# Closing norm of a two-layer recurrent decoder step: three sums into one bank and one root, a spread without a diagonal, two scalings moved behind the last sum

## Chip, core and metric

One Trainium2 chip, one of its cores. The metric is the device time of one execution in microseconds. Engines are named as in the profile: PE (TensorE matmul), PEld (its weight load), DVE (VectorE), ACT (ScalarE), POOL (GpSimd), SP (SyncE). ACTq and SPq are the queues of ACT and SP on which DMAs are issued. "L1797" is line 1797 of the kernel.

## The reference, cut to what matters

1024 prompt tokens and 8 x 4 sample tokens go through two layers of width 1024: an RG-LRU block, then an HGRN2 block. Both layers end in an output projection and a residual add, and after the second comes one more RMS norm:

```python
def _rmsnorm(x, gain):
    xf = x.astype(jnp.float32)
    y = xf * lax.rsqrt(jnp.mean(xf * xf, axis=-1, keepdims=True) + EPS)
    return (y * gain.astype(jnp.float32)).astype(x.dtype)
...
    return x + y @ w_out, S_T.astype(x.dtype)
...
    return _rmsnorm(x, final_gain), jnp.stack(hs), jnp.stack(bufs), jnp.stack(Ss)
```

The change touches only this last norm, for the last of the tokens.

## The kernel before, in words

Activations lie transposed: 128 features on the partitions, tokens along the free dimension, 1056 tokens (TOK) in a row. The width of 1024 is eight such tiles, called m (or k) = 0 to 7 below. fp32 products are made of three matmuls with operands split into a high and a low part (`mm3`, L266 to L268).

The second layer, with its output projection and the last norm, is recorded into one planner (`Flow`). Each call of `fl.add`, `act`, `dve`, `pool`, `pe` or `dma` records an operation with an engine, an estimated duration, the keys that it reads and writes and a priority. `Flow.run` then makes a list schedule, improves it by passes from the end and by a random search, and emits the operations in the order it found. Each engine then runs its own instructions strictly in that order, and waits on semaphores for the others. A DMA is issued by SP, or by ACT for odd tiles, and takes its place in that engine's order.

The projection's last three eighths of the inner dimension are done at the very end, span by span. `OUT` has three spans of tokens: 512, 288 and 256. For each span and each m:

- PE makes nine matmuls into one of three PSUM banks (`mm`);
- DVE adds that to the residual in SBUF (L1797);
- ACT squares the new x (L1799);
- the squares are summed over the eight m: for the first two spans on POOL, by adding to an accumulator (L1808). In the last span m = 1, 2 and 3 go that way, and from m = 4 on PE sums directly.

The sum over the 128 partitions is a matmul with the accumulator (or a square) as weights and one column of ones as the moving operand (`norm_sum`, L303). It gives one number for each token, with 128 tokens on the partitions. One such matmul is needed for each 128 tokens of the span, so two for the last span, each into a bank of its own. In the last span there are five rounds of them: the accumulator (m = 0 to 3), then the squares of m = 4, 5, 6 and 7.

`roots` takes a square root for each column (ACT, L1740), a reciprocal for all (DVE, L1743), and multiplies an identity by the result, so that the numbers stand on a diagonal (DVE, L1744, and L1748 for the rest that is no multiple of 128). `spread` multiplies ones by that diagonal on PE (L1754): each partition then holds the factor of every token. `finish` scales the eight tiles of x by the gain and the factor and stores them. DVE does five of them in one instruction each, from the PSUM bank (L1774). For the other three (k = 5, 6, 7) ACT copies the bank to SBUF (L1767), ACT multiplies x by the gain (L1771) and POOL by the copy (L1772). The store of each tile is a DMA (L336): even k on SP, odd k on ACT. The program lets one engine at a time read a bank of PSUM: DVE's first scaling, ACT's copy and DVE's next scaling of a span wait for one another.

The scaling of a span is placed inside the next one: its sums are made when the next span stands at m = 3 (`RM`), its spread and scaling at m = 6 (`SM`). So the 288 span is scaled while the 256 span's last products run. After the last sums two idle matmuls (`spin`, L1812) are recorded, then the roots, spread and scaling of the last span, which have nothing beside them.

In profile names, x of the last stage is `ST` for k = 0, `R` for k = 1, 2, 3, `a` (a_114) for k = 4 and `sg` (sg_147, sg_145, sg_149) for k = 5, 6, 7. The squares go to other parts of tiles `a` (a_115) and `sg` (sg_150), the accumulator is in `R`, the copy of the factors is in `sg` (sg_146), the roots are `nr`.

Of the kernel before, what the change touches and what calls it, by code (L numbers as in the profile page):

```python
# [19 lines left out]
ALU = mybir.AluOpType  # L20
# [214 lines left out]
def tile_trunk(ctx: ExitStack, tc: tile.TileContext, xT, prm, hc, w0, wg, wo0, w1, wo1, s_in,  # L235
# [64 lines left out]
    def norm_sum(sums, acc, n, start, stop):  # L300

        for s, (a, u) in zip(sums, spans(n)):
            T.matmul(s[:u], acc[:, a:a + u], ones[:, :1], start=start, stop=stop)  # L303

# [663 lines left out]
    with ExitStack() as l1:  # L968
# [787 lines left out]

        def summed(acc, ak, n):
# [5 lines left out]
        def finish(a, n, bc, bk):  # L1763
            q = slice(a, a + n)
            own = KD - 3 if a else KD
            if a:
                act(n, lambda: S.copy(sb[0][:, :n], bc), (bk,), (sb[1],), 0)  # L1767
            for k in (*range(own, KD), *range(own)):
                x, xk = x2[k][:, q], ykeys(Y2 + k, a, n)
                if k >= own:  # L1770
                    act(n, lambda x=x, k=k: S.activation(x, x, AF.Copy, scale=pc("gf", k)), xk, xk, 1)  # L1771
                    pool(n, lambda x=x: G.tensor_tensor(x, x, sb[0][:, :n], op=ALU.mult), (sb[1], *xk), xk, 1)  # L1772
                else:
                    dve(n, lambda x=x, k=k: V.scalar_tensor_tensor(x, x, pc("gf", k), bc, op0=ALU.mult, op1=ALU.mult), (bk, *xk), xk, 1)  # L1774
                dma(yT[k][:, q], x, xk, (), 1, n / 2, S if k % 2 else Q)

        for a, n in OUT:
# [4 lines left out]
            for m in range(KD):  # L1782
                if a and m == RM:
                    dg = summed(*prev[:2], prev[3])
                if a and m == SM:
                    finish(*prev[2:], *spread(prev[3], *dg, True))
# [13 lines left out]
                if final and m >= 4:  # L1800
                    if m == 4:
                        sums = [(next(hg)) for _ in spans(n)]
                        sumk = [k for _, k in sums]
                        sums = [s[:, :1] for s, _ in sums]
                        fl.add("PE", 0.3, lambda acc=acc, n=n, sums=sums: norm_sum(sums, acc, n, True, False), (ak,), sumk, 0)
                    fl.add("PE", 0.3, lambda sq=sq, n=n, m=m, sums=sums: norm_sum(sums, sq, n, False, m == KD - 1), (sk, *sumk), sumk, 0)
# [4 lines left out]
        for _ in range(2):  # L1811
            fl.add("PE", 0.45, lambda: T.matmul(spin[:, :128], ones, ones, start=True, stop=True), sumk, (wk,), 0)  # L1812
        finish(a, n, *spread(n, *roots(n, sums, sumk), False))
# [73 lines left out]
```

## Time and profile before

| what | value |
|---|---|
| median of 3 runs | 1031.88 us (1031.04 to 1032.02) |
| profiled execution, its own time | 1033.11 us |
| its span, first to last instruction | 1031.3 us |
| busy share of the span: PE, DVE, ACT, POOL | 99%, 78%, 56%, 48% |
| mean granted clock of TensorE | 0.996 |

The span leaves out what lies ahead of the first and behind the last instruction, 1.81 us in this execution. Its time is 1.23 us above the median of the runs without a profile. Busy times of PE are modelled, so 99% says that PE is seldom without a matmul, not that it is at its peak. In the rows of a timeline the columns are start, duration, engine, line, operation, what it writes and reads, its shape, and in brackets how long the engine was idle before it and what ended that. "x2" is two merged instructions; an fp32 matmul appears as two matmuls.

### The profile page before, as it was taken

How to read it: one execution, taken by the hardware profiler on the slowest of the kernel's cores; microseconds unless marked ns; L12 is line 12 of the kernel's file. 1: busy time of each engine (PE TensorE's matmuls, PEld its weight loads, DVE VectorE, ACT ScalarE, POOL GpSimd, SP SyncE). 2: the span in 40 equal slices, each digit the busy share in tenths (PEclk: the TensorE clock that was granted, in tenths of full speed). 3: DMA queues.
4: the chain of work that ended last, by engine and by line, in shares of the span. 5: the costliest groups of instructions: out<-in, count | busy, mean ns of one | idle time of the engine just before them, and what ended most of it. 6: DMA issues, size and time to landing. Idle time of an engine off the chain costs nothing.

```text
span 1031.3 us, 26510 instructions
## 1 busy us (share of the span) xinstructions
PE 1019.6 (99%) x10134; PEld 998.2 (97%) x10134; DVE 804.9 (78%) x1641; ACT 579.8 (56%) x1326; POOL 496.4 (48%) x573
## 2 busy tenths in 40 slices
PE   9999999999999999999999999999999999999997
PEld 9999999999999999999999999999999999999986
DVE  7998785779798779335598999787989798986436
ACT  8787645876765776335354373626263636552333
POOL 0216353544435255635525555555565557633544
PEclk9999999999999999999999999999999999999998
DMA  8211112223661477526564244443635353686204
GB/s 295 83 29 56 59 50 73 62 62 104 211 211 59 138 253 252 158 92 210 166 189 134 69 154 131 130 142 111 167 111 168 104 162 119 206 243 208 88 1 168
DMA packets 109582, 139.95 MB, mean 136 GB/s; under 512 B 24208, under 2 KB 86800, under 8 KB 109456
## 3 DMA queue, kind: packets, MB, share of 16 engines
q1 hardware_dynamic: 107152, 135.50, 42.8%
q10 hardware_dynamic: 2304, 2.77, 0.8%
q8 instruction: 79, 1.29, 0.5%
q14 instruction: 47, 0.39, 0.1%
HBM read 90.02 MB, written 41.61 MB: 128 GB/s over the span
## 4 chain that ended last, share of the span: by engine, by line
PE 84%; DVE 5%; ACT 4%; DMA 3%; issue 2%; SPq 1%; POOL 0%; ACTq 0%; POOLq 0%; DVEq 0%
PE mm L266 24%; PE mm L267 24%; PE mm L268 24%; PE hg L1101 2%; PE hg L266 1%; PE hg L268 1%; PE hg L267 1%; SPq L336 1%; PE hg L1248 1%; PE hg L1303 1%; DMA R<-td 1%; DMA k<-yd 1%; PE hg L1305 1%; DVE R L628 1%; DMA wraw<-in_w_dram 1%
## 5 line engine op out<-in xcount | busy, mean ns | idle before, releaser
L266 PE MATMUL mm<-xh,whi 128*128 128x352 f32 (+1 forms) x1127 | 350.2, 311 | 0.3 <-DVE k L1561 0.2
L268 PE MATMUL mm<-xh,wlo 128*128 128x352 f32 (+1 forms) x1127 | 347.5, 308 | 0.0
L267 PE MATMUL mm<-xl,whi 128*128 128x352 f32 (+1 forms) x1127 | 347.4, 308 | 0.0
L350 POOL TENSOR_TENSOR wlo<-wraw,whi 128x256 fp32r<-128x256 f32 (+3 forms) x188 | 201.7, 1090 | 210.2 <-ACT whi L409 99.9
L266 PEld LDWEIGHTS mm<-xh,whi 128*128 128x128 f32 x1127 | 212.0, 188 | 1.7 <-issue 0.4
L267 PEld LDWEIGHTS mm<-xl,whi 128*128 128x128 f32 x1127 | 212.6, 189 | 0.7 <-DVE xl L350 0.3
L268 PEld LDWEIGHTS mm<-xh,wlo 128*128 128x128 f32 x1127 | 211.8, 188 | 0.0
L266 PE MATMUL mm<-t,whi 128*128 128x264 f32 (+1 forms) x330 | 96.6, 293 | 0.0
L268 PE MATMUL mm<-t,wlo 128*128 128x264 f32 (+1 forms) x330 | 94.5, 286 | 0.0
L267 PE MATMUL mm<-t,whi 128*128 128x264 f32 (+1 forms) x330 | 94.3, 286 | 0.0
L530 DVE SCALAR_TENSOR_TENSOR k<-xb,prm_sb,k 128x352 f32<-128x352 f32 (+2 forms) x144 | 83.1, 613 | 11.5 <-ACT k L527 10.2
L1561 DVE TENSOR_TENSOR k<-mm,k 128x264 f32<-128x264 f32 x154 | 64.1, 424 | 11.7 <-PE mm L268 10.5
L350 POOL TENSOR_TENSOR wlo<-R,whi 128x256 fp32r<-128x256 f32 x70 | 57.5, 841 | 28.4 <-ACT whi L1485 25.2
L1485 ACT CAST whi<-wraw 128x512 fp32r<-128x512 f32 x56 | 34.6, 618 | 57.9 <-DVE wraw L1495 31.2
L266 PEld LDWEIGHTS mm<-t,whi 128*128 128x128 f32 x330 | 62.0, 188 | 1.3
L409 ACT CAST whi<-wraw 128x512 fp32r<-128x512 f32 (+2 forms) x79 | 43.9, 571 | 33.0 <-PE mm L267 18.0
L267 PEld LDWEIGHTS mm<-t,whi 128*128 128x128 f32 x330 | 62.2, 188 | 0.0
L268 PEld LDWEIGHTS mm<-t,wlo 128*128 128x128 f32 x330 | 62.1, 188 | 0.0
L623 POOL TENSOR_TENSOR k<-X 128x352 f32<-128x352 f32 x36 | 42.5, 1188 | 37.4 <-DVE R L624 26.9
L266 PE MATMUL mm<-yh,whi 128*128 128x352 f32 x153 | 50.0, 327 | 1.5 <-DVE k L675 0.7
L268 PE MATMUL mm<-yh,wlo 128*128 128x352 f32 x153 | 49.4, 323 | 0.0
L267 PE MATMUL mm<-yl,whi 128*128 128x352 f32 x153 | 49.4, 323 | 0.0
(465 smaller groups left out, 2513.6 us busy)
## 6 DMA issues: line engine op xcount, KB each, us to landing
wraw<-in_w_dram SPq DMA_DIRECT2D x88, 256.0 KB, 3.1
wraw<-in_wo_dram SPq DMA_DIRECT2D x34, 192.0 KB, 2.6
R<-in_w_dram SPq DMA_DIRECT2D x17, 256.0 KB, 3.3
si<-in_s_in_dram SPq DMA_DIRECT2D x8, 512.0 KB, 4.7
vt<-sg SPq DMA_DIRECT2D x8, 512.0 KB, 4.4
kt<-kt SPq DMA_DIRECT2D x8, 512.0 KB, 3.8
sg<-vt SPq DMA_DIRECT2D x32, 128.0 KB, 3.1
kt<-kt SPq DMA_DIRECT2D x32, 128.0 KB, 4.8
```

What stands on the lines that cost most here:

```text
L266: T.matmul(out, wh, xh, start=first, stop=False)
L267: T.matmul(out, wh, xl, start=False, stop=False)
L268: T.matmul(out, wl, xh, start=False, stop=last)
L336: fl.add("SP" if q is Q else "ACT", us, lambda: q.dma_start(dst, src), r, w, prio, kb * (1.0 if r else 0.75))
L350: emit = lambda: e.tensor_tensor(b, x, a.bitcast(F32), op=ALU.subtract)
L409: act(m, lambda hi=hi, raw=raw, m=m: S.copy(hi[:, :m], raw[:, :m]), rk, (hk,), prio)
L530: dve(u, lambda src=src, dst=dst, sh=sh, k=k: V.scalar_tensor_tensor(dst, sh(src, k), pc("cw", 12 * k + m), dst, op0=ALU.mult, op1=ALU.add ...
L623: pool(CH, lambda x=x, a=a, b=b: G.tensor_tensor(x, a.bitcast(F32), b.bitcast(F32), op=ALU.add), (ak, bk), (xk,), 3)
L628: dve(3 * CH, lambda ta=ta, ab=ab: V.scalar_tensor_tensor(ta, ab, 1.0, ta, op0=ALU.add, op1=ALU.mult), (*tak, *(("a", s, j) for j in range ...
L1101: T.matmul(ps[32 * j:32 * j + 32, n * w:n * w + w], B[:, o:o + 32], q(slice(o, o + 32)), start=True, stop=True, tile_position=(0, 32 * j))
L1485: act(512, lambda: S.copy(hi, raw), (rk,), (hk,), 2)
L1561: dve(QT, lambda: V.tensor_tensor(o[0], z[0], u[0], op=ALU.add), (z[1], u[1]), (o[1],), 0)
```

## The change

For the 256 span, `last_sum` replaces the five rounds of `norm_sum` by three: the accumulator now takes m = 0 to 5, so POOL adds the squares of m = 4 and 5 as well, and PE sums only the accumulator, m = 6 and m = 7. Both halves of the span go to two columns of one bank. So one square root of 128 x 2 replaces two of 128 x 1. The diagonal falls away: `spread_last` takes the column of roots itself, repeated 128 times, as weights and the identity as the moving operand, in two matmuls of 128 tokens.

In the 288 span, DVE's scalings of k = 3 and 4 are held until x of m = 7 of the 256 span has been added. For the last span POOL's three tiles are now k = 2, 3, 4 instead of 5, 6, 7. The spread's bank of the 288 span changes too, since fewer banks are taken for sums.

```diff
--- before.py
+++ after.py
@@ -302,6 +302,11 @@
         for s, (a, u) in zip(sums, spans(n)):
             T.matmul(s[:u], acc[:, a:a + u], ones[:, :1], start=start, stop=stop)
 
+    def last_sum(s, acc, n, first, last):
+
+        for i, (a, u) in enumerate(spans(n)):
+            T.matmul(s[:u, i:i + 1], acc[:, a:a + u], ones[:, :1], start=first and not i, stop=last, skip_group_check=True)
+
     def new_acts():
         hs, ls = [], []
         for k in range(KD):
@@ -1754,25 +1759,42 @@
             fl.add("PE", 0.002 * n, lambda: T.matmul(bc[:, :n], ones, dg, start=True, stop=True), (dk,), (bk,), 0, main=main)
             return bc[:, :n], bk
 
+        def spread_last(n, r, rk):
+
+            bc, bk = next(hg)
+
+            def emit():
+                for i, (a, u) in enumerate(spans(n)):
+                    T.matmul(bc[:, a:a + u], r[:, i:i + 1].to_broadcast([128, 128]), ident, start=True, stop=True)
+
+            fl.add("PE", 0.0035 * n, emit, (rk,), (bk,), 0)
+            return bc[:, :n], bk
+
         def summed(acc, ak, n):
             s, sk = next(hg)
             sums = [s[:, i:i + 1] for i in range(4)]
             fl.add("PE", 0.7, lambda: norm_sum(sums, acc, n, True, True), (ak,), (sk,), 0, main=True)
             return roots(n, sums, (sk,))
 
-        def finish(a, n, bc, bk):
+        def scaled(k, q, a, n, bc, bk, after=()):
+
+            x, xk = x2[k][:, q], ykeys(Y2 + k, a, n)
+            dve(n, lambda: V.scalar_tensor_tensor(x, x, pc("gf", k), bc, op0=ALU.mult, op1=ALU.mult), (bk, *xk, *after), xk, 1)
+            dma(yT[k][:, q], x, xk, (), 1, n / 2, S if k % 2 else Q)
+
+        def finish(a, n, bc, bk, others, now):
             q = slice(a, a + n)
-            own = KD - 3 if a else KD
-            if a:
+            own = [k for k in range(KD) if k not in others]
+            if others:
                 act(n, lambda: S.copy(sb[0][:, :n], bc), (bk,), (sb[1],), 0)
-            for k in (*range(own, KD), *range(own)):
+            for k in others:
                 x, xk = x2[k][:, q], ykeys(Y2 + k, a, n)
-                if k >= own:
-                    act(n, lambda x=x, k=k: S.activation(x, x, AF.Copy, scale=pc("gf", k)), xk, xk, 1)
-                    pool(n, lambda x=x: G.tensor_tensor(x, x, sb[0][:, :n], op=ALU.mult), (sb[1], *xk), xk, 1)
-                else:
-                    dve(n, lambda x=x, k=k: V.scalar_tensor_tensor(x, x, pc("gf", k), bc, op0=ALU.mult, op1=ALU.mult), (bk, *xk), xk, 1)
+                act(n, lambda x=x, k=k: S.activation(x, x, AF.Copy, scale=pc("gf", k)), xk, xk, 1)
+                pool(n, lambda x=x: G.tensor_tensor(x, x, sb[0][:, :n], op=ALU.mult), (sb[1], *xk), xk, 1)
                 dma(yT[k][:, q], x, xk, (), 1, n / 2, S if k % 2 else Q)
+            for k in own[:now]:
+                scaled(k, q, a, n, bc, bk)
+            return lambda after: [scaled(k, q, a, n, bc, bk, after) for k in own[now:]]
 
         for a, n in OUT:
             q = slice(a, a + n)
@@ -1783,7 +1805,7 @@
                 if a and m == RM:
                     dg = summed(*prev[:2], prev[3])
                 if a and m == SM:
-                    finish(*prev[2:], *spread(prev[3], *dg, True))
+                    rest = finish(*prev[2:], *spread(prev[3], *dg, True), (5, 6, 7) if prev[2] else (), 3 if final else KD)
                 ps, pk = next(mm)
                 hi, lo, wk = late[m]
 
@@ -1797,20 +1819,23 @@
                 dve(n, lambda x=x, ps=ps, n=n: V.tensor_tensor(x, ps[:, :n], x, op=ALU.add), (pk, *xk), xk, 0)
                 sq, sk = next(sqs) if m else (acc, ak)
                 act(n, lambda sq=sq, x=x, n=n: S.activation(sq[:, :n], x, AF.Square), xk, (sk,), 1)
-                if final and m >= 4:
-                    if m == 4:
-                        sums = [(next(hg)) for _ in spans(n)]
-                        sumk = [k for _, k in sums]
-                        sums = [s[:, :1] for s, _ in sums]
-                        fl.add("PE", 0.3, lambda acc=acc, n=n, sums=sums: norm_sum(sums, acc, n, True, False), (ak,), sumk, 0)
-                    fl.add("PE", 0.3, lambda sq=sq, n=n, m=m, sums=sums: norm_sum(sums, sq, n, False, m == KD - 1), (sk, *sumk), sumk, 0)
+                if final and m >= 6:
+                    if m == 6:
+                        sums, sumk = next(hg)
+                        fl.add("PE", 0.45, lambda acc=acc, n=n, sums=sums: last_sum(sums, acc, n, True, False), (ak,), (sumk,), 0)
+                    fl.add("PE", 0.45, lambda sq=sq, n=n, m=m, sums=sums: last_sum(sums, sq, n, False, m == KD - 1), (sk, sumk), (sumk,), 0)
                 elif m:
                     pool(n, lambda acc=acc, sq=sq, n=n: G.tensor_tensor(acc[:, :n], acc[:, :n], sq[:, :n], op=ALU.add), (sk, ak), (ak,), 1)
             prev = acc, ak, a, n
         spin, wk = next(mm)
         for _ in range(2):
-            fl.add("PE", 0.45, lambda: T.matmul(spin[:, :128], ones, ones, start=True, stop=True), sumk, (wk,), 0)
-        finish(a, n, *spread(n, *roots(n, sums, sumk), False))
+            fl.add("PE", 0.45, lambda: T.matmul(spin[:, :128], ones, ones, start=True, stop=True), (sumk,), (wk,), 0)
+        rest(ykeys(Y2 + KD - 1, a, n))
+        w = n // 128
+        r, rk = next(nr2)
+        act(4, lambda: S.activation(r[:, :w], sums[:, :w], AF.Sqrt, bias=epsc, scale=1.0 / D), (sumk,), (rk,), 0)
+        dve(16, lambda: V.reciprocal(r[:, :w], r[:, :w]), (rk,), (rk,), 0)
+        finish(a, n, *spread_last(n, r, rk), (2, 3, 4), KD)
         with tc.manual_schedule(engines={E.PE, E.DVE, E.Activation, E.Pool, E.SP}):
             fl.run(SEARCH, 60.0)
 
```

Everything ahead of the 288 span's scaling stands in the same order as before on all engines, apart from one memset of four columns that falls away on DVE and the order of two DMA issues and an ACT scaling. The order at the end does change, in three places.

On ACT, from the last span's square of m = 5 to the root, before. L1799 are the squares (of sg_147, sg_145, sg_149: m = 5, 6, 7), L1771 the gain on POOL's tiles, L336 the stores of the 288 span (R_73: k = 1 and 3, sg: k = 5 and 7), L1740 the roots:

```order
L1799 ACTIVATE a_115<-sg_147 128x256
L1767 COPY sg_146<-mm_158 128x288
L1771 ACTIVATE sg_147<-sg_147,prm_sb_74 128x256
L336 DMA out_yT_dram<-R_73 128x288
L336 DMA out_yT_dram<-sg_147 128x288
L1799 ACTIVATE a_115<-sg_145 128x256
L1771 ACTIVATE sg_145<-sg_145,prm_sb_74 128x256
L336 DMA out_yT_dram<-R_73 128x288
L1799 ACTIVATE sg_150<-sg_149 128x256
L1771 ACTIVATE sg_149<-sg_149,prm_sb_74 128x256
L336 DMA out_yT_dram<-sg_149 128x288
L1740 ACTIVATE nr20_5315<-hg_164,eps_85 128x1
```

The same stretch of ACT now, where L1821 are the squares, L1789 the copy, L341 the stores and L1836 the root:

```order
L1821 ACTIVATE a_115<-sg_147 128x256
L1789 COPY sg_146<-hg_164 128x288
L341 DMA out_yT_dram<-R_73 128x288
L1821 ACTIVATE a_115<-sg_145 128x256
L341 DMA out_yT_dram<-sg_147 128x288
L1821 ACTIVATE sg_150<-sg_149 128x256
L341 DMA out_yT_dram<-R_73 128x288
L341 DMA out_yT_dram<-sg_149 128x288
L1836 ACTIVATE nr20_5315<-hg_161,eps_85 128x2
```

The three gain scalings have left this stretch (they stand earlier, for k = 2, 3, 4), and one store fewer stands ahead of the square of m = 6. The stores of k = 3 and k = 7 still stand between the last square and the root.

On DVE, from the add of m = 6 (sg_145) to the first scaling of the last span, before. L1797 are the adds, L1774 the scalings:

```order
L1797 TENSOR_TENSOR sg_145<-mm_160,sg_145 128x256
L1774 SCALAR_TENSOR_TENSOR R_73<-R_73,prm_sb_74,mm_158 128x288
L1774 SCALAR_TENSOR_TENSOR a_114<-a_114,prm_sb_74,mm_158 128x288
L1797 TENSOR_TENSOR sg_149<-mm_157,sg_149 128x256
L1743 RECIPROCAL nr20_5315<-nr20_5315 128x2
L1744 TENSOR_TENSOR sg_150<-ident_75,nr20_5315 128x256
L1774 SCALAR_TENSOR_TENSOR ST_143<-ST_143,prm_sb_74,hg_162 128x256
```

And DVE now, with L1819 for the adds and L1782 for the scalings:

```order
L1819 TENSOR_TENSOR sg_145<-mm_160,sg_145 128x256
L1819 TENSOR_TENSOR sg_149<-mm_157,sg_149 128x256
L1782 SCALAR_TENSOR_TENSOR R_73<-R_73,prm_sb_74,hg_164 128x288
L1782 SCALAR_TENSOR_TENSOR a_114<-a_114,prm_sb_74,hg_164 128x288
L1837 RECIPROCAL nr20_5315<-nr20_5315 128x2
L1782 SCALAR_TENSOR_TENSOR ST_143<-ST_143,prm_sb_74,mm_158 128x256
```

The add of m = 7 has moved ahead of two scalings of the 288 span, and the diagonal between reciprocal and scaling is gone.

On POOL, from the last add of the last span to its scalings, before, with L1808 for the adds of squares and L1772 for the scalings:

```order
L1808 TENSOR_TENSOR R_73<-R_73,sg_150 128x256
L1808 TENSOR_TENSOR R_73<-R_73,a_115 128x256 x2
L1772 TENSOR_TENSOR sg_147<-sg_147,sg_146 128x288
L1772 TENSOR_TENSOR sg_145<-sg_145,sg_146 128x288
L1772 TENSOR_TENSOR sg_149<-sg_149,sg_146 128x288
```

And POOL now, with L1828 for the adds and L1793 for the scalings:

```order
L1828 TENSOR_TENSOR R_73<-R_73,sg_150 128x256
L1828 TENSOR_TENSOR R_73<-R_73,a_115 128x256 x2
L1828 TENSOR_TENSOR R_73<-R_73,sg_150 128x256
L1828 TENSOR_TENSOR R_73<-R_73,a_115 128x256
L1793 TENSOR_TENSOR sg_147<-sg_147,sg_146 128x288
L1793 TENSOR_TENSOR sg_145<-sg_145,sg_146 128x288
L1793 TENSOR_TENSOR sg_149<-sg_149,sg_146 128x288
```

Two adds of squares, m = 4 and 5, now stand ahead of the three scalings of the 288 span.

## Prediction

> **What bounds the kernel now.** I read the page first, then the end of the chain, the waits, the timelines of the five engines for the last 15 us, and the granted clock in short stretches.
>
> ```profile
> span 1031.3 us, 26510 instructions
> PE 1019.6 (99%) x10134; PEld 998.2 (97%) x10134; DVE 804.9 (78%) x1641; ACT 579.8 (56%) x1326; POOL 496.4 (48%) x573
> 1019.18 2.32 POOL sg L1772 x3
> 1021.50 3.94 issue
> POOL sg L1772 <- ACT sg L1767: 5.8, 2, 4.0
> ```
>
> PE bounds the kernel up to its last product. The change leaves all of that alone, so only what follows can move. The chain (third and fourth row) leads back through POOL, which "issue" shows doing nothing for 3.94 us. The wait beneath shows for whom: ACT's copy of the spread factors. So the true chain must be read from the timelines: last product, add, square, sum, roots, diagonal, spread, copy, scalings, stores.
>
> PE, then DVE, at the end (idle time and its releaser in brackets):
>
> ```profile
> 1017.46 0.65 PE L1754 MATMUL mm<-sg,ones 128*128 128x288 f32 x2
> 1019.96 0.28 PE L268 MATMUL mm<-t,xl 128*128 128x256 f32 x1
> 1022.15 0.61 PE L303 MATMUL hg<-ones,sg 128*128 128x1 f32 x4 [0.23 <-ACT sg L1799]
> 1022.62 0.69 PE L1812 MATMUL mm<-ones 128*128 128x128 f32 x4
> 1023.77 1.22 PE L1754 MATMUL hg<-sg,ones 128*128 128x256 f32 x2 [0.46 <-DVE sg L1744]
> 1019.99 0.42 DVE L1797 TENSOR_TENSOR sg<-mm,sg 128x256 f32<-128x256 f32 x1
> 1020.32 0.51 DVE L1774 SCALAR_TENSOR_TENSOR R<-R,prm_sb,mm 128x288 f32<-128x288 f32 x1
> 1020.74 0.51 DVE L1774 SCALAR_TENSOR_TENSOR a<-a,prm_sb,mm 128x288 f32<-128x288 f32 x1
> 1021.17 0.42 DVE L1797 TENSOR_TENSOR sg<-mm,sg 128x256 f32<-128x256 f32 x1
> 1023.09 0.17 DVE L1743 RECIPROCAL nr<-nr 128x2 f32<-128x2 f32 x1 [1.50 <-ACT nr L1740]
> 1023.29 0.42 DVE L1744 TENSOR_TENSOR sg<-ident,nr 128x256 f32<-128x256 f32 x1
> 1025.43 0.48 DVE L1774 SCALAR_TENSOR_TENSOR ST<-ST,prm_sb,hg 128x256 f32<-128x256 f32 x1 [1.72 <-ACT sg L1767]
> ```
>
> The last product ends at 1019.96 + 0.28 = 1020.24, but its add starts only at 1021.17: two scalings of the 288 span stand ahead of it. That is 0.9 us on the chain. Reciprocal to scaling takes 2.3 us, of which the diagonal is 0.42 and the spread 1.22. The earlier spread, of more columns (288), took 0.65: the late one runs at half speed. The granted clock (the 1.00, 0.88 and 0.50 behind the five engines' pairs) shows why:
>
> ```profile
> 1023.50:1023.60 0.10, 0.00 (x0) 0.00 (x0) 0.10 (x1) 0.00 (x0) 0.00 (x0) 1.00 0.11 23
> 1023.60:1023.65 0.05, 0.00 (x0) 0.00 (x0) 0.05 (x1) 0.00 (x0) 0.00 (x0) 0.88 0.00 0
> 1023.65:1023.70 0.05, 0.00 (x0) 0.00 (x0) 0.05 (x1) 0.00 (x0) 0.00 (x0) 0.50 0.00 0
> ```
>
> 0.88 over 0.05 us puts the fall to one half at 1023.64, 0.13 ahead of the spread and 3.40 behind the last product.
>
> ACT, its queue, and POOL:
>
> ```profile
> 1018.18 0.42 ACT L1799 ACTIVATE a<-sg 128x256 f32<-128x256 f32 x1 [0.64 <-DVE sg L1797]
> 1018.70 0.40 ACT L1767 COPY sg<-mm 128x288 f32<-128x288 f32 x1
> 1020.11 0.39 ACTq L336 DMA_DIRECT2D out_yT_dram<-sg  x1
> 1020.55 0.42 ACT L1799 ACTIVATE a<-sg 128x256 f32<-128x256 f32 x1 [1.04 <-DVE sg L1797]
> 1021.00 0.51 ACT L1771 ACTIVATE sg<-sg,prm_sb 128x256 f32<-128x256 f32 x1
> 1021.68 0.42 ACT L1799 ACTIVATE sg<-sg 128x256 f32<-128x256 f32 x1 [0.18 <-DVE sg L1797]
> 1022.19 0.34 ACTq L336 DMA_DIRECT2D out_yT_dram<-sg  x1
> 1022.58 0.48 ACT L1740 ACTIVATE nr<-hg,eps 128x1 f32<-128x1 f32 x2
> 1025.02 0.37 ACT L1767 COPY sg<-hg 128x256 f32<-128x256 f32 x1 [1.97 <-PE hg L1754]
> 1016.63 0.74 POOL L1808 TENSOR_TENSOR R<-R,a 128x256 f32<-128x256 f32 x1 [0.59 <-ACT a L1799]
> 1019.18 2.32 POOL L1772 TENSOR_TENSOR sg<-sg 128x288 f32<-128x288 f32 x3 [1.81 <-ACT sg L1767]
> 1025.47 2.09 POOL L1772 TENSOR_TENSOR sg<-sg 128x256 f32<-128x256 f32 x3 [3.98 <-ACT sg L1767]
> ```
>
> A store's issue holds ACT's next instruction: the square at 1020.55 follows the issue that ends at 1020.50, and the roots at 1022.58 follow one that ends at 1022.53.
>
> **The change part by part.** I follow the chain and write the new time beside the old; the last is what the term is worth so far.
>
> *Add and square of m = 7.* The add stands right behind that of m = 6, whose successor started 0.33 behind it (1020.32 - 1019.99). Its product is ready at 1020.24. So it runs from 1020.32 to 1020.74: 0.85 earlier. Its square doesn't gain all of that. The square of m = 6 loses the store ahead of it and starts 0.09 behind its add (as 1021.68 stands 0.09 behind 1021.59), at 1020.50, and ends at 1020.92. Behind it one store is issued (0.39), so I put the square of m = 7 at 1021.00 to 1021.42, against 1021.68 to 1022.10: **0.68**.
>
> *The added wait.* The scalings of k = 3 and 4 now run from 1020.66 to 1021.6 at their old pitch. Nothing on DVE stands behind them before the reciprocal. The store of k = 3 waits on ACT for the first, done at 1021.17, with the root queued behind: it can issue while the square runs, so this costs nothing. SP's store of k = 4 goes 0.3 later, with 4 us to the next stores.
>
> *Two adds more on POOL.* Each costs 0.74. The square of m = 5 ends at 1018.60, so its add ends about 1019.40 and the three 288 scalings end 0.18 later than before, at 1021.68 instead of 1021.50. The store of k = 7 waits for the third, and the root stands behind this store: 1021.72 + 0.34, root from about 1022.11. What hid the adds is POOL's idle time (1.81 ahead of the scalings); if POOL is later still, the root is later one for one.
>
> *Sums and root.* The sums of m = 7 start 0.05 behind their square and take 0.61: 1021.47 to 1022.08. The one root waits for both halves, where the first of two could start after one half; one of 128 x 2 should take the 0.24 of each of the two. So it ends at about 1022.13 + 0.26 = 1022.39 against 1023.06: **0.67**. "One root" alone is worth nothing here: half a sum (about 0.3 of the 0.61) is waited for in its place. A reading of two columns could cost less or more than one of the two old roots by no more than that 0.24, so the term is bounded by 0.24 on either side. The sums left out were hidden: those of m = 4 and 5 ran ahead of the wait for m = 7.
>
> *Diagonal.* Reciprocal at 1022.42 to 1022.59; the spread follows 0.06 behind instead of 0.51 (1023.26 to 1023.77): 1022.65, **1.12** in all. The spin ends about 0.66 earlier too, at 1022.65, and is not in the way.
>
> *Spread.* Two matmuls of 128 columns in place of one of 256: the same columns, two more weight loads. The nearest row at full clock with these shapes is the spin, 0.69 for four pieces; the nearest at half clock is 1.22. I take 0.66, since it runs 1.0 us ahead of where the clock fell. It ends at 1023.31 instead of 1024.99: **1.68**. At half clock it is 1.22 to 1.30, and the sum 1.04 to 1.12.
>
> [...]
>
> *Copy, scalings, stores.* The copy starts the last stage as before. DVE still does five tiles and POOL three, in other tiles. Its rows and the stores:
>
> ```profile
> 1025.94 0.33 SPq L336 DMA_DIRECT2D out_yT_dram<-ST  x1
> 1027.64 0.41 SPq L336 DMA_DIRECT2D out_yT_dram<-a  x1
> 1027.78 0.41 ACTq L336 DMA_DIRECT2D out_yT_dram<-sg  x1
> 1022.00:1023.50 1.50, 1.16 (x8) 0.97 (x8) 0.38 (x2) 1.02 (x4) 0.00 (x0) 1.00 0.98 337
> 1023.50:1024.00 0.50, 0.23 (x1) 0.24 (x2) 0.21 (x1) 0.00 (x0) 0.00 (x0) 0.64 0.02 5
> 1027.00:1028.00 1.00, 0.00 (x0) 0.00 (x0) 0.47 (x2) 0.00 (x0) 0.56 (x1) 0.50 0.98 321
> ```
>
> The first store is issued 0.55 behind the copy's end, the last 2.4 behind. In between the DMA engines are full (last numbers: share 0.98, 321 GB/s), so the stage's end follows its first issue. The 288 span's stores are through by 1023.5 (share 0.02 after it); up to 0.4 later, they still miss the new stores. I count zero, within 0.1 either way. The gain scalings of k = 2 to 4 sit in ACT's gaps of about 0.64 ahead of each square; at 0.51 each they fit, with 0.1 to spare.
>
> **Sum:** 1.68, rounded down to 1.6 for the closeness of POOL's store and the root. The profiled execution of 1033.11 would become 1031.5, its span 1029.7. That execution stands 1.23 above the median, so I carry the difference: 1031.88 - 1.6 = 1030.3.
>
> **The rivals.**
>
> *The spread stays at half clock.* The fall came 3.40 behind the last product in this execution; if it comes under 2.4 behind it in others, the whole spread is slow, and the gain is 1.05: 1030.8. For it speaks that PE now has four sums fewer between last product and spread; against it that PE was idle for only 0.23 there and the clock still 1.00 at 1023.6. [...]
>
> *POOL holds the root.* The store of k = 7 stands ahead of the root and the slack is nil. One POOL operation of delay, 0.8, moves root and spread by as much, and the spread's end past 1023.64, some 0.4 more: gain 0.4, 1031.5. For it speaks that the two adds are new there; against it that POOL's rows are steady.
>
> *Weights from a repeated column are slow.* PE now loads weights from one column read 128 times, of which no row has an example. A load has 0.19:
>
> ```profile
> L303 PEld LDWEIGHTS hg<-ones,sg 128*128 128x128 f32 x8 | 1.0, 191 | 0.3 <-ACT sg L1799 0.3
> ```
>
> There are four. If each took 0.41 longer the gain would be gone; at 1 us each they add 3.2 and the kernel is slower by 1.6, 1033.5. Against it: DVE's diagonal also read a repeated column and took 0.42, as a plain add of that size.
>
> *More than that.* If the 0.9 us in front of the last add came back whole, with no store ahead of square or root, the root would end 0.17 earlier and the gain would be about 1.9; over 2.06 it needs a share that no row shows.
>
> **How the numbers follow.** 0.2% of 1031.88 is 2.06 us, about what a measurement of this kernel can tell from no change. Forecast (full clock, 1.2 to 2.0): 0.60. Half clock: 0.17. POOL: 0.10. Slow weights: 0.05, most of it slower by over 2.06 or near. More than 2.06: 0.08. All but the last two lie within 0.2%. With some of the forecast's upper edge, faster gets 0.13, slower 0.05, same 0.82. The range takes in half clock and POOL above, and the upper edge below: 1029.6 to 1031.6.
>
> **What would show it.** Right: the add of m = 7 some 0.1 behind the last product's end; about 2.4 us from that end to the reciprocal's (3.0 before); a spread of about 0.66 at clock 1.00; the copy about 3.1 behind the last product instead of 4.8. Wrong: a clock of 0.50 in the spread, the root right behind a store's issue well after its sums, a long weight load, or stores that start earlier but end no earlier.

## The result and the profile after

| | before | after |
|---|---|---|
| median, 21 runs each | 1031.28 us (1028.9 to 1033.07) | 1029.71 us (1028.48 to 1031.13 in 20) |
| profiled execution, its own time | 1033.11 us | 1029.22 us |
| its span | 1031.3 us | 1027.4 us |

The ratio is 0.9987, with a 95% interval of 0.9981 to 0.9992: a gain of 1.3 us (0.8 to 2.0), less than the 2.06 us (0.2%) up to which the forecast counts a change as none. The medians differ by 1.57 us. Three runs far off the others are left out: one after of 2433.79 us, and below one of e11 of 2442.81 us and one of the kernel before of 2545.52 us. A later set of 11 runs (below) gave 0.9991 (0.9982 to 1.0000), or 0.9 us. The forecast was 1030.3 and a gain of 1.6.

The two profiled executions differ by 3.9 us, more than twice that. To see how much of it is the change, I split the execution at the end of the last product, called E below. The page after:

```profile
span 1027.4 us, 26498 instructions
PE 1016.6 (99%) x10128; PEld 996.5 (97%) x10128; DVE 802.7 (78%) x1639; ACT 580.4 (56%) x1325; POOL 499.9 (49%) x575
```

PE is as busy as before, and POOL has its two adds more. From the chain of the last 10 us (start, length, what):

```profile
1019.33 2.15 issue
```

This stretch, in which POOL stands and the true chain runs elsewhere, went from 3.94 to 2.15. The timelines of PE, DVE, ACT, POOL and SP there:

```profile
1017.55 0.28 PE L268 MATMUL mm<-t,xl 128*128 128x256 f32 x1
1018.56 0.61 PE L308 MATMUL hg<-ones,a 128*128 128x1 f32 x4 [0.39 <-ACT a L1821]
1019.02 0.60 PE L308 MATMUL hg<-ones,sg 128*128 128x1 f32 x4
1019.49 0.69 PE L1832 MATMUL mm<-ones 128*128 128x128 f32 x4
1020.26 0.71 PE L1768 MATMUL mm<-ident,nr 128*128 128x128 f32 x4
...
1017.57 0.75 DVE L1819 TENSOR_TENSOR sg<-mm,sg 128x256 f32<-128x256 f32 x2
1020.04 0.17 DVE L1837 RECIPROCAL nr<-nr 128x2 f32<-128x2 f32 x1 [0.87 <-ACT nr L1836]
...
1018.55 0.42 ACT L1821 ACTIVATE sg<-sg 128x256 f32<-128x256 f32 x1
1018.78 0.34 ACTq L341 DMA_DIRECT2D out_yT_dram<-R  x1
1019.37 0.34 ACTq L341 DMA_DIRECT2D out_yT_dram<-sg  x1
1019.75 0.26 ACT L1836 ACTIVATE nr<-hg,eps 128x2 f32<-128x2 f32 x1 [0.78 <-PE hg L308]
1021.07 0.37 ACT L1789 COPY sg<-mm 128x256 f32<-128x256 f32 x1 [1.05 <-PE mm L1768]
...
1016.33 0.74 POOL L1828 TENSOR_TENSOR R<-R,a 128x256 f32<-128x256 f32 x1 [0.32 <-ACT a L1821]
1017.02 2.31 POOL L1793 TENSOR_TENSOR sg<-sg 128x288 f32<-128x288 f32 x3
...
1021.98 0.33 SPq L341 DMA_DIRECT2D out_yT_dram<-ST  x1
```

E is 1017.55 + 0.28 = 1017.83. Both adds of the last two products now run in one go (x2), the square of m = 7 starts at 0.72 behind E, the root at 1.92, the spread at 2.43, and the copy ends at 3.61. Before, the same points were 1.44, 2.34, 3.53 and 5.15 behind its E of 1020.24. From the copy's end to the end of the span it takes 5.97 (1027.41 - 1021.44), against 5.94. So the tail, from E to the end of the span, went from 11.09 to 9.58: **1.5 us is the change's**. The other 2.4 us lie ahead of E.

They don't come from the change. The row with which the 512 span's products start, before and after:

```profile
982.05 0.39 PE L266 MATMUL mm<-t,xh 128*128 128x512 f32 x1
```

```profile
979.63 0.39 PE L266 MATMUL mm<-t,xh 128*128 128x512 f32 x1
```

From that product to E it takes 38.19 and 38.20 us, and 38.19 to 38.20 in all thirteen profiles that the study can use. Where it starts scatters from 978.14 to 983.32, ahead of anything that the change touches (two other profiles of these kernels, one of each, had 980.44 and 981.28). A pair of profiled executions can't measure a change of 1 us here; the tail, which repeats within 0.01, can.

The granted clock (first of the last three numbers) at the fall:

```profile
1021.55:1021.60 0.05, 0.00 (x0) 0.00 (x0) 0.05 (x1) 0.00 (x0) 0.05 (x1) 1.00 0.00 0
1021.60:1021.65 0.05, 0.00 (x0) 0.00 (x0) 0.05 (x1) 0.00 (x0) 0.05 (x1) 0.53 0.00 0
```

It falls at 1021.60, 3.77 behind E, when the spread has long been done.

### The profile page after: what moved, and what is told of

Same layout as the page of the kernel before. It is cut to its first block, busy times and chain, and to the rows that moved or that the text cites. A ratio compares the mean times of both kernels' runs of the same rounds, so it can differ in the third digit from the quotient of the medians.

```text
span 1027.4 us, 26498 instructions
## 1 busy us (share of the span) xinstructions
PE 1016.6 (99%) x10128; PEld 996.5 (97%) x10128; DVE 802.7 (78%) x1639; ACT 580.4 (56%) x1325; POOL 499.9 (49%) x575
## 4 chain that ended last, share of the span: by engine, by line
PE 93%; DVE 3%; DMA 2%; issue 1%; POOL 0%; ACT 0%; SPq 0%; ACTq 0%; POOLq 0%; DVEq 0%
PE mm L266 27%; PE mm L267 26%; PE mm L268 26%; PE hg L1106 2%; PE hg L266 1%; PE hg L268 1%; PE hg L267 1%; PE hg L1253 1%; PE hg L1308 1%; DMA wraw<-in_w_dram 1%; PE hg L1310 1%; DMA sg<-in_xT_dram 1%; PE mm L1253 1%; PE hg L1283 0%; PE mm L1106 0%
```

## The experiments

The forecast's account is a sum of steps: the hold of two scalings, the diagonal and a spread that now ends ahead of the clock's fall carry the gain, one root and fewer sums bring nothing. Against it stood that the fall is not counted from the last product, so that the spread's share is chance, and that the steps are not worth their rows one by one. The expectations give each side's numbers. All are kernels with one edit (e1 and e9 with none, e10 with two), seen in one profile each; those that were also timed are named. Times are us behind the kernel's own E.

| kernel | its time | reciprocal | spread: start, length | copy ends | tail | clock falls |
|---|---|---|---|---|---|---|
| before | 1033.11 | 2.85 | 3.53, 1.22 | 5.15 | 11.09 | 3.40 |
| after | 1029.22 | 2.21 | 2.43, 0.71 | 3.61 | 9.58 | 3.77 |
| e1 before again | 1031.49 | 2.85 | 3.53, 1.22 | 5.15 | 11.09 | 2.84 |
| e2 no hold | 1033.96 | 2.78 | 3.05, 1.17 | 4.69 | 10.67 | 2.60 |
| e3 diagonal back | 1030.72 | 2.23 | 2.91, 0.70 | 4.07 | 10.05 | 4.49 |
| e4 two roots | 1031.26 | 2.38 | 2.60, 1.22 | 4.23 | 10.21 | 2.39 |
| e5 before with hold | 1031.09 | 2.46 | 3.14, 0.70 | 4.25 | 10.19 | 4.28 |
| e6 five rounds | 1030.33 | 2.51 | 2.73, 0.71 | 3.90 | 9.88 | 4.66 |
| e7 stores on SP | 1028.26 | 2.11 | 2.33, 0.71 | 3.52 | 9.51 | 5.49 |
| e8 two spreads | 1030.47 | 2.23 | 2.45, 0.71 | 4.07 | 9.22 | 5.73 |
| e9 after again | 1030.84 | 2.22 | 2.44, 0.71 | 3.61 | 9.59 | 3.90 |
| e10 e7 and e8 | 1027.43 | 2.11 | 2.33, 0.78 | 4.45 | 9.32 | 2.84 |

**e1: the kernel before, once more, no edit.** Does the clock fall at the same place?

> The kernel before, unchanged, once more. All times of this study are counted from the end of the last product, which was followed by 5.15 us to the end of ACT's copy of the factors and by 11.06 us to the end of the span in the first profile. Theory A (the gain of the change is three terms: 0.68 from the earlier add of m = 7, 0.45 from the diagonal, 0.5 from a spread at full instead of half clock; the rest of the difference between the two profiles lies ahead of the last product and is scatter): the clock falls at about 3.4 us again, the spread takes 1.22 us and the copy ends at 5.15. Theory B (the clock falls at the end of whole windows whose phase differs from execution to execution, so the slow spread of the first profile was an accident of phase): the clock falls anywhere between 3.4 and 6.8, the spread most likely takes 0.6 us, and the copy ends at 4.5 to 4.6. Then the change is worth about 1.0 us in most executions and 1.5 in a few.

The clock in short stretches, then the spread in PE's timeline:

```profile
1021.40:1021.45 0.05, 0.05 (x3) 0.05 (x1) 0.00 (x0) 0.04 (x1) 0.00 (x0) 1.00 0.66 208
1021.45:1021.50 0.05, 0.05 (x3) 0.05 (x1) 0.02 (x1) 0.00 (x0) 0.00 (x0) 0.71 1.08 369
```

```profile
1022.16 1.22 PE L1754 MATMUL hg<-sg,ones 128*128 128x256 f32 x2 [0.37 <-DVE sg L1744]
```

With E at 1018.63 the fall is 2.84 behind it, not 3.40: it isn't counted from the last product. Nor did it come between 3.4 and 6.8, as theory B has it. It fell while the spin ran (1021.01 to 1021.79). The work itself repeats to 0.01, slow spread included.

**e2: without the hold.**

```diff
-                    rest = finish(*prev[2:], *spread(prev[3], *dg, True), (5, 6, 7) if prev[2] else (), 3 if final else KD)
+                    rest = finish(*prev[2:], *spread(prev[3], *dg, True), (5, 6, 7) if prev[2] else (), KD)
```

> The changed kernel, but the two scalings of the 288 span are not held behind the add of m = 7; they stand ahead of it, as before. The changed kernel has the copy's end at 3.61 us behind the last product and the span's end at 9.57. Theory A: the add of m = 7 starts at 0.93 instead of 0.07, its square ends 0.6 to 0.7 later, and the copy ends at 4.25 to 4.3 (with the spread at full clock; up to 0.5 more if the clock falls ahead of it). Rival: the root was held by the store of k = 7 and POOL, not by its sums, so most of the earlier add was worth nothing; the copy ends at 3.7 or less.

DVE's and ACT's timelines:

```profile
1021.59 0.50 DVE L1782 SCALAR_TENSOR_TENSOR R<-R,prm_sb,hg 128x288 f32<-128x288 f32 x1
1022.01 0.51 DVE L1782 SCALAR_TENSOR_TENSOR a<-a,prm_sb,hg 128x288 f32<-128x288 f32 x1
1022.44 0.41 DVE L1819 TENSOR_TENSOR sg<-mm,sg 128x256 f32<-128x256 f32 x1
...
1022.89 0.42 ACT L1821 ACTIVATE sg<-sg 128x256 f32<-128x256 f32 x1 [0.70 <-DVE sg L1819]
```

The two scalings stand ahead of the last add again, and the reciprocal comes 0.57 later (2.78 against 2.21). The copy ends 1.08 later; of that 0.46 is a slow spread, since the clock fell at 2.60. So the hold is worth 0.57 in this order.

**e3: the diagonal back.**

```diff
-        finish(a, n, *spread_last(n, r, rk), (2, 3, 4), KD)
+        dg, dk = next(dgs)
+        dve(n, lambda: V.tensor_tensor(dg[:, :n].rearrange("p (i n) -> p i n", i=w), ident[:, None, :].to_broadcast([128, w, 128]),
+                                       r[:, :w, None].to_broadcast([128, w, 128]), op=ALU.mult), (rk,), (dk,), 0)
+        finish(a, n, *spread(n, dg[:, :n], dk, False), (2, 3, 4), KD)
```

> The changed kernel, but the factors of the last span are put on a diagonal by DVE again and spread by one matmul of 256 columns. Theory A: the diagonal adds 0.45 to 0.5 us; one matmul of 256 columns takes 0.60 instead of the 0.71 of two with 128 each, so the copy ends at 3.95 to 4.0 instead of 3.61 if the clock holds. Rival: the two loads of a repeated column and the shorter matmuls cost as much as the diagonal; the copy ends at 3.6 to 3.7. A fall of the clock ahead of the spread would add 0.5 to either and shows in the granted clock.

DVE's and PE's rows:

```profile
1021.29 0.43 DVE L1839 TENSOR_TENSOR sg<-ident,nr 128x256 f32<-128x256 f32 x1
...
1021.77 0.70 PE L1759 MATMUL mm<-sg,ones 128*128 128x256 f32 x2 [0.56 <-DVE sg L1839]
```

The copy ends at 4.07 instead of 3.61: the diagonal is worth 0.46. At full clock the old spread from two matmuls of 256 takes 0.70, the new from four pieces of 128 takes 0.71: the form costs nothing, and the column that is read 128 times as weights costs nothing either (its four loads take 0.52 in the changed kernel, the spin's 0.53).

**e4: two roots, two banks.** The two halves are summed into a bank each, by `norm_sum` (L303).

```diff
...
-        act(4, lambda: S.activation(r[:, :w], sums[:, :w], AF.Sqrt, bias=epsc, scale=1.0 / D), (sumk,), (rk,), 0)
+        for i in range(w):
+            act(4, lambda i=i: S.activation(r[:, i:i + 1], sums[i], AF.Sqrt, bias=epsc, scale=1.0 / D), (sumk[i],), (rk,), 0)
```

> The changed kernel, but the sums of the two halves go to two banks and ACT takes two roots of 128 x 1. Theory A with the store ahead of the root: in the changed kernel the store of k = 7 was issued until 1.88 us behind the last product and the root started at 1.92, when both sums were done at 1.79, so two roots one behind the other end 0.22 later, at 2.4, and the copy ends at 3.8. Rival (the forecast's own step: one root is worth nothing, since the first of two roots can start after half of the sums): the copy ends at 3.6.

ACT and PE, then the clock:

```profile
1020.82 0.34 ACTq L341 DMA_DIRECT2D out_yT_dram<-sg  x1
1021.21 0.26 ACT L1838 ACTIVATE nr<-hg,eps 128x1 f32<-128x1 f32 x1 [0.79 <-PE mm L303]
1021.37 0.25 ACT L1838 ACTIVATE nr<-mm,eps 128x1 f32<-128x1 f32 x1
...
1020.71 0.36 PE L303 MATMUL mm<-ones,sg 128*128 128x1 f32 x2
1021.87 1.22 PE L1768 MATMUL hg<-ident,nr 128*128 128x128 f32 x4 [0.25 <-DVE nr L1839]
```

```profile
1021.65:1021.70 0.05, 0.00 (x0) 0.00 (x0) 0.05 (x1) 0.00 (x0) 0.00 (x0) 0.62 1.07 346
```

The second half's sum ends at 1021.07 (1020.71 + 0.36), and the first root comes only at 1021.21, behind the store's issue that ends at 1021.16 (the row names PE, which had been done for 0.14). Both roots then follow one another: the reciprocal is 0.17 later, so one root instead of two is worth 0.17. And here the new spread is slow, 1.22 from 2.60, for the clock fell at 2.39: the forecast's rival of the half clock, here in one execution.

**e5: the kernel before with the hold alone** (k = 3 and 4 of the 288 span behind the add of m = 7).

```diff
+                    if hold and k in (3, 4):
+                        continue
...
+        rest(ykeys(Y2 + KD - 1, a, n))
```

> The kernel before with one part of the change alone: the scalings of k = 3 and 4 of the 288 span are held behind the add of m = 7. In the kernel before (first profile and second alike) the square of m = 7 started 1.44 us behind the last product and the copy ended at 5.15, with a slow spread. Theory A: the square starts at 0.75, everything up to the spread moves by 0.65 to 0.7, the spread starts at 2.85; the copy ends at 4.5 with a slow spread (1.22 us) and at 3.9 with one at full clock (0.60). Rival: with the gain scalings of k = 5 to 7 still in ACT's order and the store of k = 7 ahead of the roots, the roots move by 0.3 or less; the copy ends at 4.85 or at 4.25.

ACT and PE:

```profile
1019.78 0.51 ACT L1771 ACTIVATE sg<-sg,prm_sb 128x256 f32<-128x256 f32 x1
1020.20 0.40 ACT L1809 ACTIVATE sg<-sg 128x256 f32<-128x256 f32 x1
...
1019.78 1.03 PE L303 MATMUL hg<-ones,a 128*128 128x1 f32 x8
1020.67 0.58 PE L303 MATMUL hg<-ones,sg 128*128 128x1 f32 x4
```

The hold alone brings 0.39 (2.46 against 2.85), not 0.57. The gain scaling of k = 6 stands ahead of the square of m = 7, and PE is still at the sums of m = 5 and 6 when that square ends: both had been hidden by the late add. The other parts of the change clear both away.

**e6: five rounds of sums in the new form.**

```diff
-                if final and m >= 6:
-                    if m == 6:
+                if final and m >= 4:
+                    if m == 4:
```

> The changed kernel, but the last span's squares of m = 4 and 5 are summed by PE again (five rounds into the one bank) and not added by POOL. Theory A: these sums lie ahead of the wait for m = 7 and cost nothing, and POOL's three scalings of the 288 span end 0.2 to 0.3 earlier, so that the store of k = 7 no longer holds the root (which starts 0.13 behind the sums in the changed kernel): the copy ends at 3.5 to 3.6 with the spread at full clock, 4.1 with a slow one. Rival: fewer rounds were what the change lived on, PE's sums of m = 6 and 7 come later behind the additional ones, and the copy ends at 3.9 or later at full clock.

PE and ACT:

```profile
1019.31 1.03 PE L308 MATMUL hg<-ones,a 128*128 128x1 f32 x8
1020.20 0.58 PE L308 MATMUL hg<-ones,sg 128*128 128x1 f32 x4
...
1020.88 0.26 ACT L1836 ACTIVATE nr<-hg,eps 128x2 f32<-128x2 f32 x1 [0.98 <-PE hg L308]
```

With E at 1018.66 the sums of m = 7 start at 1.54 instead of 1.19, behind eight pieces that follow one another every 0.11. Root and reciprocal are 0.30 later. So leaving out two rounds is worth 0.30 here, where the forecast had nothing. (The planner also put ACT's stores in another order. The last issue ends at 2.16 and the sums at 2.12, so the issue accounts for 0.06 of the root's 2.22 at most.)

**e7: the odd stores of the 288 span issued by SP**, so that none stands ahead of ACT's square and root.

```diff
-            dma(yT[k][:, q], x, xk, (), 1, n / 2, S if k % 2 else Q)
+            dma(yT[k][:, q], x, xk, (), 1, n / 2, S if k % 2 and a != OUT[1][0] else Q)
...
```

> The changed kernel, but all eight stores of the 288 span are issued by SP, so that none stands between ACT's squares and the root. Theory A: the square of m = 7 starts at 0.65 to 0.7 instead of 0.72, the root within 0.05 of the end of the sums instead of 0.13, so the copy ends 0.1 us earlier, at 3.5, with the spread at full clock (4.05 with a slow one). Rival: the stores on ACT cost nothing; 3.6 (4.15).

ACT:

```profile
1017.57 0.42 ACT L1821 ACTIVATE sg<-sg 128x256 f32<-128x256 f32 x1
1018.79 0.26 ACT L1836 ACTIVATE nr<-hg,eps 128x2 f32<-128x2 f32 x1 [0.81 <-PE hg L308]
```

Square at 0.59 instead of 0.72, root at 1.81 instead of 1.92, copy 0.09 earlier, tail 0.07 shorter. The issues on ACT cost about 0.1, no more: the last sums start at 1.19 as before, behind the sums of m = 6, although the square is done earlier.

**e8: a second spread into a bank of its own for ACT's copy**, so that DVE's first scaling doesn't wait for the copy.

```diff
...
-        finish(a, n, *spread_last(n, r, rk), (2, 3, 4), KD)
+        first = spread_last(n, r, rk)
+        finish(a, n, *first, (2, 3, 4), KD, spread_last(n, r, rk, first[1]))
```

> The changed kernel, but the spread is made twice, into two banks: DVE scales from the first as soon as it is there, and ACT copies the second for POOL. In the changed kernel DVE's first scaling started 0.50 us behind the end of the spread, behind ACT's copy, and the span ended 9.58 us behind the last product. Theory A (the last stage's end follows its first store, since the DMA engines are full from then on): the first scaling starts 0.1 behind the first spread and the first store 0.4 earlier; POOL starts 0.4 to 0.5 later, which the queue of stores hides; the span ends at 9.2 with spreads at full clock, 9.8 with slow ones. Rival: POOL's three tiles, now later, set the end; 9.6 or more at full clock.

DVE and PE, then the clock:

```profile
1022.67 0.48 DVE L1782 SCALAR_TENSOR_TENSOR ST<-ST,prm_sb,mm 128x256 f32<-128x256 f32 x1 [0.80 <-PE mm L1768]
...
1022.47 0.61 PE L1768 MATMUL hg<-ident,nr 128*128 128x128 f32 x4
```

```profile
1021.70:1021.90 0.20, 0.12 (x2) 0.00 (x0) 0.17 (x1) 0.00 (x0) 0.00 (x0) 1.00 1.04 340
1025.15:1025.20 0.05, 0.00 (x0) 0.00 (x0) 0.00 (x0) 0.00 (x0) 0.05 (x1) 0.98 1.05 369
1025.20:1025.25 0.05, 0.00 (x0) 0.00 (x0) 0.00 (x0) 0.00 (x0) 0.05 (x1) 0.50 1.01 348
```

DVE now waits for PE, not for ACT, and starts at 3.20 instead of 3.64. The copy is 0.46 later, yet the tail is 0.36 shorter, for the first store is issued 0.44 earlier (3.71 against 4.15): the stage's end follows its first store, as the forecast read it. The clock rows come back below.

**e9 and e10: the changed kernel again, and both of e7's and e8's edits,** timed in one set against the kernel before (20 runs, median 1030.87).

> The changed kernel once more, unchanged, for a second profile and more times beside the next one. Theory C, formed from the profiles so far: the clock falls at the end of a free-running window of 3.41 us that holds less than about 1.1 us of dense products, so 2.35 to 5.77 us behind the last product, evenly spread; the changed kernel's spread (2.43 to 3.14) is slowed in one execution in five, the one before (from 3.53) in one of two, wholly or partly. So the change is worth 1.0 us at equal clock and 1.15 on average: a ratio of 0.9989. In the profile the copy ends at 3.61 if the clock falls behind 3.1, and the span 9.58 behind the last product. Rival (the fall is tied to the last product at 3.4 us, or the bulk ahead of the last product has gained too): a ratio of 0.9985 or less.

> The changed kernel with both additions: the 288 span's stores all on SP, and the spread made twice so that DVE starts without waiting for ACT's copy. Theory: the gains add, 0.09 and 0.36; at full clock DVE's first scaling starts at 3.1 and the span ends 9.13 us behind the last product (9.58 in the changed kernel); 1.45 us below the kernel before at equal clock, a ratio of 0.9985 on average. Rival: with the stores of both spans on SP closer together the last stage's stores start no earlier, and the span ends at 9.2 or later.

e9: 1029.67 in 11 runs, ratio 0.9991 (0.9982 to 1.0000); its tail repeats to 0.01. e10: 1028.06 in 10 runs, ratio 0.9979 (0.9970 to 0.9989), with a median below those of both kernels. Its two spreads on PE:

```profile
1018.66 0.78 PE L1768 MATMUL mm<-ident,nr 128*128 128x128 f32 x4
1019.23 1.06 PE L1768 MATMUL hg<-ident,nr 128*128 128x128 f32 x4
```

The clock fell at 2.84, so the second spread took 1.06 instead of 0.61, and the copy and POOL behind it came late: a tail of 9.32 where 9.13 was expected. That is the rival's number for another reason than the rival's: the first store came at 3.65, earlier and not later. The profile is not typical of its runs. In six of the ten the mean clock is 0.999 or more, which leaves 3.1 us at half clock at most (2 x 1026 x 0.0015). There the fall comes 6 us or more behind E, behind both spreads, and the tail should be nearer to 9.13, as an estimate.

e10's median is 1.6 below e9's, and its tail only 0.3. This, and an early start of the 512 span in e7 and e10 (978.79 and 978.14, the earliest two), raised the question whether moving the stores also saves time ahead of the tail. e7 and e8 were therefore timed, together.

> The kernel with the 288 span's odd stores issued by SP, now timed. Only the tail counts (first theory): its tail is 0.1 us shorter than that of the changed kernel, so its time should be about 1029.6 beside 1029.7 of the changed kernel, and the product from which the 512 span starts (978.8 us in its earlier profile) should fall anywhere from 978 to 983.5 as in the others. Moving the stores also takes time out ahead of the 512 span (second theory, which would explain why this kernel and the one with both edits had the two earliest starts of twelve): about 1028.4, with a start of the 512 span again near 978 to 979.

> The kernel with a second spread for ACT, now timed. First theory (only the tail counts): 0.36 us shorter than the changed kernel, about 1029.3. Second theory (the stores' move, which this kernel lacks, saves about 1.2 us ahead of the 512 span): the same 1029.3 here, so about 0.9 us above the kernel with the stores on SP instead of 0.3 below it.

e11: 1029.55 in 12 runs, ratio 0.9983 (0.9968 to 0.9998). e12: 1029.20 in 12 runs, ratio 0.9978 (0.9964 to 0.9992), with a tail of 9.21. The first theory's 1029.6 and 1029.3 fit; the second's 1028.4 for e11, below e12, does not. What bears on it is that e11 lies 0.35 above e12 in the same set, where the first has 0.3 above and the second 0.9 below. Against other sets such differences say little: the kernel before had 1031.78 in this one and 1030.87 in that of e9, and the changed kernel was not timed in it. e10's further microsecond is then scatter ahead of the tail as far as these runs tell; the intervals are too wide to exclude some of it. e11's profile is of its run of 2442.81 us, so it can't show where its 512 span starts.

## Why the prediction was right, and where it wasn't

The class and the mechanism were right: the path runs from the last add through square, sums, root and spread to the copy, and no other path set the end. The median of 1029.71 lies only 0.1 above the lower end of the range, though. By its steps:

- **Add, square, added wait.** Add at 0.07 behind its product's end (1017.57 + 0.75 - 0.42; 0.08 forecast), square at 0.72 (0.76). The wait cost nothing: DVE's two scalings were done long before the reciprocal.
- **Two adds on POOL.** They fit ahead of the 288 scalings, which end 1.50 behind E (1.44 forecast, 1.26 before). The slack for the root was nil, as said: sums done at 1.79, root at 1.92, behind the issue of the store of k = 7 (1019.37 + 0.34, 1.88 behind E). e7 prices all of ACT's issues at 0.09.
- **Sums and root.** The root ends at 2.18 (2.15 forecast). But two sentences under this step failed. "The sums left out were hidden" held only while the last add was late: e6 shows 0.30 for them. And "one root alone is worth nothing" left out that the store holds the first root until both halves are summed: e4 shows 0.17. Neither moved the total, because the forecast built the new order from its own rows, where both were already absent; they misled only about what each part is worth.
- **Diagonal.** The spread starts 1.10 earlier (1.12 forecast); the diagonal itself is 0.46.
- **Spread.** This is the term that was mis-sized. In this pair it saved 0.51 (0.56 forecast), so the pair's tail agrees with the sum: 1.5 of 1.6. But 1.22 for the old spread was taken as its usual length. The old spread takes 0.70 at full clock (e5), and at equal clock the copy would have ended at 5.15 - 0.52 = 4.63 before, 1.02 later than after. The rest is chance, by where the clock falls.
- **Copy, scalings, stores.** Zero forecast, 0.03 lost. The copy also starts 0.1 behind the spread's end where it was 0.03 before. What takes that 0.06 is open.

How often the old spread was slow: the falls that the table lists lie spread between 2.39 and 5.73 behind E. Say they are even over one step of 3.41 us, from about 2.35 to 5.77. The step is that of the last section; with 1.02 us of dense products in it the clock fell in e4, with 1.09 it stayed in e8, and I put the edge between them, at about 1.05, which is an estimate from these two alone. Then the old spread (3.53 to 4.23 at full clock) is slow whole in (3.53 - 2.35) / 3.41 = 0.35 of the executions and in part in 0.21; the new (2.43 to 3.14) whole in 0.02 and in part in 0.21. With 0.52 for a whole one and half of it for a part, the old loses 0.24 on average, the new 0.06. The gain to expect is 1.02 + 0.18 = 1.2 us, as an estimate. The runs put it rather higher. In 28 of the 42 runs of the kernel before that the sets of e9 and e11 keep, the mean clock is 0.996 or less. If it fell once, that is at least 7.2 us at half clock (2 x 1029.5 x 0.0035), so by the tail of 11.09 a fall within 3.9 of E. The even spread has less than half of them there ((3.9 - 2.35) / 3.41 = 0.45). So the old spread was slow more often than estimated. In five of the 28, at 0.995 or less, one fall would have to lie ahead of 1.9, which no profile shows; what else slowed them is open. The two measurements, 1.3 (0.8 to 2.0) and 0.9 (0 to 1.9), agree with 1.2 and with more; they don't tell 1.0 from 1.6.

- **Rivals.** Slow weights: the four loads take 0.52 for the spread and 0.53 for the spin. POOL in front of the root: true as to the order, but about 0.1 instead of 0.8 (the root stands 0.13 behind its sums, in e7 0.04). Half clock: seen whole in e2 and e4 and in part in e10; a part of executions and not a case of its own. More than that: with no store ahead of square and root, e7 gains 0.09 and not the 0.17 of the forecast.
- The forecast of 1030.3 lies 0.6 above the median: the three runs it started from had a median 0.6 above that of the 21 (1031.88 and 1031.28). By the medians the gain was the 1.6 that was forecast; by the ratio it was 1.3, and by the tails at equal clock 1.0, so part of that agreement is chance.

The parts don't add up: taken out of the finished order one by one they are worth 0.57, 0.30, 0.17 and 0.46, together 1.50, but the whole is 1.02 at equal clock. Hold, rounds and root each get in the other's way, so the last one removed seems to bring it all, and the first alone (e5) brings less.

## What to carry to other kernels

Price a part of a change in the order that results, not in the old one: what is hidden behind a late instruction (sums, a gain scaling, a store's issue) becomes the bound when that instruction comes early, and parts that look worthless alone are what lets another part pay. Compare two profiles from a point that both share, here the end of the last dense product, since the executions ahead of it differ by more than the change. And when a duration rests on the granted clock, look at that clock in a second execution before booking the difference as a gain.

## What the runs showed of the hardware

**The clock's fall isn't counted from the last product.** In the trace's record of the granted clock, the stretch at full clock is 1017.172 us long in ten of the thirteen profiles (before, after, e1 to e7 and e9), with E anywhere from 1016.98 to 1021.51. It is 1020.585 in e8 and e12, and 1013.758 in e10: 3.41 more and 3.41 less (298, 299 and 297 times 3.4133). So in these profiles the full clock ended on one of a row of steps of 3.41 us, wherever the work stood. That decides against a fall counted from the last product. What sets the steps was not shown.

**Dense products in the last step don't settle it.** e4's last step, from 1.02 ahead of E to 2.39 behind it, held 1.02 us of dense products, the sums of one column and the spin, and the clock fell at its end. In e8 the clock falls at 1025.20; one step earlier, at 1021.79, it stays at 1.00 (first of e8's clock rows), with 1.09 us of dense products in that step, the same sums and the spin but for its last 0.03. Theory C of e9 puts the edge at about 1.1 us, as these two would have it. But e12, with two spreads behind the spin, fell only at 7.65:

```profile
1024.00:1027.50 3.50, 0.00 (x0) 0.00 (x0) 1.17 (x3) 0.00 (x0) 2.10 (x3) 1.00 0.83 277
1027.50:1027.60 0.10, 0.00 (x0) 0.00 (x0) 0.00 (x0) 0.00 (x0) 0.00 (x0) 0.89 0.97 352
```

Its step from 0.83 to 4.24 held no dense product at all, only sums, spin and the two spreads, and the clock stayed at 1.00; at the end of the changed kernel's, from 0.36 to 3.77, with the same sums and spin and one spread, it fell. So 1.1 us of dense products is not what it takes to stay. Nor does PE's modelled busy time tell the steps apart: e1's last (1018.06 to 1021.47) has 3.18 us of it and the clock fell, e12's (1020.76 to 1024.17) 2.68 and it stayed. What decides was not shown.

The timed runs differ in the same way: with the second spread the mean clock is 0.999 or 1.0 in nine of e12's twelve runs and in six of e10's ten; in the 31 runs of the changed kernel it is 0.998 at most.
